# A hybrid convolution and gMLP trunk on eight cores: another DMA queue for cached weights, write-backs in mid-use, a norm pipelined with mixer A, conv weights on VectorE

## The chip, the cores and the metric

The program runs on all 8 cores of one Trainium2 chip; each core works on its own 4096 tokens, and nothing is exchanged between cores. The metric is the device time of the slowest core, in microseconds (us). Executions in a slow state (one die, cores 0 to 3 or 4 to 7, at a lower granted clock, or a run over 1.5% above the fastest of its kernel) are set aside; only fast runs are compared. TensorE is called PE.

A core does its tokens in four passes (0 to 3) of 1024. A pass has a layer 0 mixer, an MLP, a layer 1 mixer and an MLP. The weights, 45 pieces of 1 MB in bf16, come through a ring of four slots in every pass. The first load of a piece is a cast load: GpSimd issues a DMA that reads 2 MB of float32 and writes 1 MB of bf16. The piece is then written back to a bf16 cache in device memory, and later loads take it from there.

Four marks are used throughout; unless said otherwise each is the median of the eight cores in the profiled execution:

- *conv end*: the last matmul of mixer A's convolution in pass 0
- *late stretch*: from the first matmul of layer 0's output projection in pass 0 to the first projection matmul of pass 1
- *pass 0 end*: that first projection matmul of pass 1
- *pass 1 stretch*: from there to pass 1's own layer 0 output projection

## The reference, cut to what matters

```python
def conv_mixers(h, w_in, ...):                      # layer 0
    z = h @ w_in                                    # one projection, 2560 columns
    a = a_val * sigmoid(a_gate)                     # A: GLU
    a = silu(layer_norm(causal_depthwise_conv(a, conv_a_w) + conv_a_b))   # width 31
    bo = b_gate * causal_depthwise_conv(c_gate * b_val, conv_b_w)         # B
    return concatenate([a, bo]) @ w_out
for i in range(2):
    h = h + mixer_i(rms_norm(h))                    # layer 0 above, layer 1 gMLP
    h = h + squared_relu_mlp(rms_norm(h))
return rms_norm(h)
```

## The kernel before

The kernel records every operation with what it reads and writes; waits follow from that record, and each engine runs its own operations in order. SyncE issues all DMAs except the cast loads.

```python
NEV = 7
def wb_mt(i):                       # pass in which piece i is written back
    return 1 if i % NPIECE < NEV else 0     # layer 0's seven "ev" pieces: pass 1
def issue(i, gate=()):
    ...
    if i // NPIECE > wb_mt(i):      # from the cache, SyncE
        P.op("sp", ... dma_start(out=ring[s], in_=wcache[...]), ...)
        return
    P.op("pool", ... dma_start(out=ring[s], in_=src), reads=list(gate), ...)   # cast load
def take(expect):                   # first use of a piece
    ...
    if i // NPIECE == wb_mt(i) and ...:
        P.op("sp", ... dma_start(out=wcache[...], in_=ring[s]), ...)           # write-back
def release(i):                     # a slot's last use is past
    issue(i + NSLOT)
...
# mixer A, group m: two token halves, then an exchange through device memory
def a_glu(m):
    for s in range(2):
        bg = fm_group(slot, cb, s); bv = fm_group(slot, cb + 1, s)    # 8 matmuls each
        ... sigmoid on ScalarE, product on VectorE into abuf[m % 2] ...
    P.op("sp", ... dma_start(out=scr_a[m]..., in_=ab.v...), dma=f"a{m}")        # store
    P.op("sp", ... dma_start(out=A4.v[...], in_=scr_a[m]...), dma=f"b{m}")      # load
...
for m in range(4):
    a_glu(m)
    if mt == 0:
        for g in range(8 + 2 * m, 10 + 2 * m): gen_cw("dve", g)   # conv weights 8 to 15
    if m % 2 == 1: release(a_pc[m // 2][0])                       # loads pieces 4 and 5
for gp in range(NG // 2): conv_pair(gp)                           # conv on PE
...   # B mixer; the normalised A output goes through scr_s the same way (4 stores)
...
for k in range(1, NSLOT):            # start: pieces 1 to 3
    issue(k, h_keys(2 * k + 1))      # each after an x tile has landed
    for g in range(3 * k - 3, min(3 * k, 8)): gen_cw("pool", g)   # conv weights 0 to 7
```

The first norm runs over all eight token tiles before the first projection; each tile's transpose comes two tiles after its scaling (LAG = 2). In both exchanges a store to device memory is followed by a load in another order; the loads of the later one (scr_s) are called gathers.

Of the kernel before, what the change touches and what calls it, by code (L numbers as in the profile page):

```python
# [18 lines left out]
NTB = 8  # L19
# [196 lines left out]
def build_program(n_mt=4):  # L216
# [16 lines left out]
    NPIECE = 45  # L233
    NEV = 7
    wcache = nc.dram_tensor("wcache", [NPIECE, 128, 8 * 512], BF16, kind="Internal").ap()

    P = Prog()
    with contextlib.ExitStack() as es:
# [93 lines left out]

        def wb_mt(i):
            return 1 if i % NPIECE < NEV else 0

        def issue(i, gate=()):
            if i >= len(pieces):
                return
            assert i == issued[0]
            issued[0] += 1  # L340
            wn, r0, c0 = pieces[i]
            s = i % NSLOT
            if i // NPIECE > wb_mt(i):
                src = wcache[i % NPIECE].rearrange("p (kc n) -> p kc n", kc=8)
                P.op("sp", lambda e, s=s, src=src: e.dma_start(out=ring[s][:], in_=src),
                     reads=[("wc", i % NPIECE)], writes=[("w", s)], dma=f"v{s}")
                return
            src = W[wn][r0:r0 + 1024, c0:c0 + 512].rearrange("(kc p) n -> p kc n", p=128)
            P.op("pool", lambda e, s=s, src=src: e.dma_start(out=ring[s][:], in_=src),
                 reads=list(gate), writes=[("w", s)], dma=f"w{s}")  # L350

        def take(expect):
            i = cur[0]
            assert pieces[i] == expect, (pieces[i], expect)
            assert i < issued[0], (i, issued[0])
            cur[0] += 1
            s = i % NSLOT
            if i // NPIECE == wb_mt(i) and i + NPIECE < len(pieces):
                dst = wcache[i % NPIECE].rearrange("p (kc n) -> p kc n", kc=8)
                P.op("sp", lambda e, s=s, dst=dst: e.dma_start(out=dst, in_=ring[s][:]),  # L360
                     reads=[("w", s)], writes=[("wc", i % NPIECE)], dma=f"wb{s}")
            return i, s

        def release(i):
            issue(i + NSLOT)
# [24 lines left out]
        for tb in range(NTB):  # L390
            load_x(0, tb)
            if tb == 3:
                P.op("sp", lambda e: e.dma_start(out=wexp.v, in_=wexp_d.rearrange("p (g u) -> p g u", g=NG)),
                     writes=wexp.k(), dma="c1")
        P.op("sp", lambda e: e.dma_start(out=cst[:], in_=bigc[:, 0:2048]), writes=[("cst",)], dma="c2")

# [9 lines left out]

        def gen_cw(eng, g):
            small(eng, lambda e: e.tensor_tensor(
                out=cw[:, g, :].rearrange("p (u c) -> p u c", c=32),
                in0=mask32.v.unsqueeze(1).to_broadcast([128, NLAG * NPH, 32]),  # L410
                in1=wexp.v[:, g, :].unsqueeze(2).to_broadcast([128, NLAG * NPH, 32]), op=ALU.mult),
                mask32.k() + wexp.ki(g), [("cw", g)])
# [57 lines left out]

        LAG = 2
        xn_done = [False]
# [6 lines left out]
        def xn_op(c0, tb, eng="act", src=h_tile, dst=xn_tile):  # L479
            (ap, keys), (out, okeys) = src(tb), dst(tb)  # L480
            col = st[:, c0 + 8 + tb:c0 + 9 + tb]
            if eng == "act":
                small("act", lambda e: e.activation(out=out, in_=ap, func=AF.Copy, scale=col),  # L483
                      keys + [("st", c0 + 8 + tb)], okeys)
            else:
                small("dve", lambda e: e.tensor_scalar(out=out, in0=ap, scalar1=col, scalar2=None, op0=ALU.mult),
                      keys + [("st", c0 + 8 + tb)], okeys)
# [46 lines left out]
        def norm_to_xnT(nidx):  # L534
# [3 lines left out]
            c0 = stcol(16)  # L538
            for tb in range(3):
                stat_tb(c0, tb)  # L540
            LATE = 6
            for tb in range(NTB):
                if tb >= LAG:
                    tr_op(nidx, tb - LAG)
                if tb >= LATE:
                    stat_tb(c0, tb)
                rstd_tb(c0, tb)
                if tb + 3 < LATE:
                    stat_tb(c0, tb + 3)
                xn_op(c0, tb, "act" if tb % 2 == 0 else "dve")  # L550
            for tb in range(NTB - LAG, NTB):
                tr_op(nidx, tb)

        pre_c0 = [0]
# [114 lines left out]
        def fm_group(slot, m, s):  # L669
# [4 lines left out]
            def mm(e):  # L674
# [3 lines left out]
                return r  # L678
            P.op("pe", mm, reads=[("w", slot)] + [("xnT", tb) for tb in range(4 * s, 4 * s + 4)], writes=[("ps", b)])
            pump()  # L680
            return b

        def tm_group(slot, lhs, lhs_keys, tb):
            b = next_bank()

            def mm(e):
# [3 lines left out]
                return r  # L690
            P.op("pe", mm, reads=[("w", slot)] + lhs_keys, writes=[("ps", b)])
            return b

# [43 lines left out]
        def mixer0(mt):  # L737
# [8 lines left out]

            def a_glu(m):
                ab = abuf[m % 2]
                slot = a_pc[m // 2][1]
                cb = 2 * (m % 2)  # L750
                for s in range(2):
                    bg = fm_group(slot, cb, s)
                    bv = fm_group(slot, cb + 1, s)
                    sg = gbuf[s]
                    small("act", lambda e, bg=bg, sg=sg: e.activation(out=sg.v, in_=banks[bg][:], func=AF.Sigmoid),
                          [("ps", bg)], sg.k())
                    small("dve", lambda e, bv=bv, sg=sg, ab=ab, s=s: e.tensor_tensor(
                        out=ab.v.rearrange("p (j q t) -> p j q t", j=NPH, q=2)[:, :, s, :],
                        in0=banks[bv][:].rearrange("p (j t) -> p j t", j=NPH),
                        in1=sg.v.rearrange("p (j t) -> p j t", j=NPH), op=ALU.mult),  # L760
                        [("ps", bv)] + sg.k(), [k for j in range(NPH) for k in ab.k(j * TP + s * 128, j * TP + s * 128 + 128)])
                P.op("sp", lambda e, ab=ab, m=m: e.dma_start(
                    out=scr_a[m].rearrange("(i c) (d t) -> (c d) i t", i=NPH, d=4),
                    in_=ab.v.rearrange("p (i t) -> p i t", i=NPH)), reads=ab.k(), writes=[("scra", m)], dma=f"a{m}")
                P.op("sp", lambda e, m=m: e.dma_start(
                    out=A4.v[:, 4 * m:4 * m + 4, HB:HB + TP], in_=scr_a[m].rearrange("p (d t) -> p d t", d=4)),
# [142 lines left out]

            for m in range(4):  # L910
                a_glu(m)
                if mt == 0:
                    for g in range(8 + 2 * m, 10 + 2 * m):
                        gen_cw("dve", g)
                if m % 2 == 1:
                    release(a_pc[m // 2][0])
            for gp in range(NG // 2):
                conv_pair(gp)
                if mt > 0 and gp >= 2:
                    load_x(mt, gp - 2)  # L920
# [130 lines left out]
        for k in range(1, NSLOT):  # L1051
            issue(k, h_keys(2 * k + 1))
            for g in range(3 * k - 3, min(3 * k, 8)):
                gen_cw("pool", g)
        for mt in range(n_mt):
# [71 lines left out]
```

## Time and profile before

| | before |
|---|---|
| three runs before the prediction | 2749.64 us median (2747.91 to 2750.39) |
| PE busy, slowest core | 2645.0 of 2745.2 us |
| first projection matmul, conv end | 49.2, 97.7 us |
| late stretch, pass 0 end | 573.2, 719.9 us (714.2 to 733.8) |
| pass 1 stretch | 108.5 us |

The profiled core is the slowest, core 1. The first lines of its page:

```profile
span 2745.2 us, 40038 instructions; the slowest of 8 cores (2726.8 to 2745.2 us)
...
PE 2645.0 (96%) x13400; PEld 1261.3 (46%) x13400; DVE 1062.3 (39%) x1949; ACT 905.5 (33%) x1625; POOL 714.3 (26%) x691
```

PE is the bottleneck; a change that leaves its own work as it is can win only its 100 idle us. The windows view tells where they are. Its columns are the window, its length, then busy time and count of PE, PE weight loads, VectorE, ScalarE and GpSimd, then PE's granted clock, DMA share and GB/s:

```profile
0.00:200.00 200.00, 141.01 (x759) 73.46 (x760) 111.54 (x158) 70.63 (x126) 42.14 (x41) 0.95 0.63 121
...
700.00:900.00 200.00, 180.32 (x985) 91.40 (x984) 108.08 (x165) 71.93 (x134) 34.12 (x29) 0.97 0.61 161
1380.00:1600.00 220.00, 215.34 (x1161) 107.81 (x1159) 116.39 (x181) 75.44 (x139) 33.87 (x29) 1.00 0.37 125
```

The start loses 59 us (200 less 141), the mixer of pass 1 20, the same mixer of pass 2 only 5. The timeline of PE shows what it waited for (start, length, instruction, and in brackets the idle time before it and its releaser):

```profile
50.01 29.07 PE L676 MATMUL bank<-xnT,ring 128*128 128x512 bf16 x128
78.91 11.99 PE L776 MATMUL bank<-Z,cw 128*128 128x256 bf16 x108
93.41 5.76 PE L776 MATMUL bank<-Z,cw 128*128 128x256 bf16 x36 [2.51 <-DMA Z<-scr_a]
...
163.04 8.09 PE L626 MATMUL bank<-ring,Z 128*128 128x512 bf16 x24 [10.27 <-DMA Z<-scr_s]
...
771.93 6.18 PE L776 MATMUL bank<-Z,cw 128*128 128x256 bf16 x36 [10.29 <-DMA Z<-scr_a]
```

Mixer A's projections run without a break from 50.0 to 78.9, conv waits 2.5 us for the exchange, the output projection of pass 0 waits 10.3 us for the second exchange (scr_s), and conv of pass 1 waits 10.3 us. One VectorE operation in the first norm stands out in the timeline:

```profile
27.13 11.39 DVE L486 TENSOR_SCALAR xn_tm<-h,st 128x1024 bf16<-128x1024 f32 x1
```

The same operation elsewhere takes 0.75 us. GpSimd was building conv weights meanwhile. Here is the exchange of mixer A, groups 0, 1 and 3, in SyncE's timeline. A load into Z waits for its store to land, so the distance from a store's line to its load's line is the time of the store:

```profile
59.31 0.38 SPq L762 DMA_DIRECT2D scr_a<-Z  x1
61.75 0.61 SPq L765 DMA_DIRECT2D Z<-scr_a  x1
66.20 0.38 SPq L762 DMA_DIRECT2D scr_a<-Z  x1
71.70 0.53 SPq L765 DMA_DIRECT2D Z<-scr_a  x1
...
80.12 0.56 SPq L762 DMA_DIRECT2D scr_a<-Z  x1
90.11 0.53 SPq L765 DMA_DIRECT2D Z<-scr_a  x1
```

A store of 256 KB took 2.4 us once and 10.0 us another time. GpSimd's timeline has a cast load issued just ahead of the slow one:

```profile
79.63 0.87 POOL L349 DMA_DIRECT2D ring<-ev_w_out  x1 [12.88 <-PE bank L676]
```

### The profile page before, as it was taken

The page shows a single profiled execution, that of the slowest core. Times are in us where ns is not written, and L with a number is a line of the kernel's source. Part 1 is how long each engine was busy: PE and PEld are TensorE (multiplying, and loading weights), DVE is VectorE, ACT ScalarE, POOL GpSimd, SP SyncE. Part 2 cuts the span into 40 slices and gives each one's busy share as a digit, 9 for nine tenths or more (in the row PEclk, how much of TensorE's full clock was granted, in tenths as well). Part 3 has the DMA queues.
Part 4 walks back from the last instruction along what each step waited for, and adds up shares of the span by engine and source line. Part 5 has one row for each costly group of instructions (what it writes and reads, how often), then busy time and mean ns, then how long its engine had stood idle before and what let it go on. Part 6 is the DMA issues. An engine that isn't in the chain of part 4 may idle for free.

```text
span 2745.2 us, 40038 instructions; the slowest of 8 cores (2726.8 to 2745.2 us)
## 1 busy us (share of the span) xinstructions
PE 2645.0 (96%) x13400; PEld 1261.3 (46%) x13400; DVE 1062.3 (39%) x1949; ACT 905.5 (33%) x1625; POOL 714.3 (26%) x691
## 2 busy tenths in 40 slices
PE   3989999999979999999999999999999999999998
PEld 2534444444444444444445444444445444445443
DVE  4641226421455123732157321462125721265223
ACT  2432135423334113532323412552333422164112
POOL 3115322323211322222311223123320133203222
PEclk9999999999999999999999999999999999999999
DMA  7567765978774211223244112122326222212212
GB/s 155 85 135 149 156 140 124 188 163 166 173 181 158 76 63 71 84 93 116 82 143 166 62 67 88 62 86 101 107 77 214 80 91 77 77 62 77 77 62 93
DMA packets 128681, 303.89 MB, mean 111 GB/s; under 512 B 22880, under 2 KB 92512, under 8 KB 106208
## 3 DMA queue, kind: packets, MB, share of 16 engines
q1 hardware_dynamic: 74400, 246.79, 25.2%
q0 software_dynamic: 54080, 54.53, 14.3%
q8 instruction: 112, 1.84, 0.3%
q14 instruction: 89, 0.73, 0.1%
HBM read 283.47 MB, written 72.35 MB: 130 GB/s over the span
## 4 chain that ended last, share of the span: by engine, by line
PE 89%; DMA 4%; DVE 3%; issue 3%; ACT 1%; SPq 0%; DVEq 0%; ACTq 0%
PE bank L688 42%; PE bank L676 41%; DMA scr_a<-Z 2%; PE bank L496 2%; PE bank L776 2%; PE bank L626 1%; DMA scr_s<-Z 1%; DMA h<-x 1%; DVE Z L896 1%; DMA Z<-scr_s 1%; PE bank L998 1%; DVE Z L826 0%; DVE Z L905 0%; DMA Z<-scr_a 0%; DVE Z L824 0%
## 5 line engine op out<-in xcount | busy, mean ns | idle before, releaser
L676 PE MATMUL bank<-xnT,ring 128*128 128x512 bf16 x5888 | 1291.3, 380 | 11.4 <-DVE Z L905 8.5
L688 PE MATMUL bank<-ring,Z 128*128 128x512 bf16 x4928 | 1080.8, 379 | 0.0
L695 DVE TENSOR_TENSOR h<-bank,h 128x512 f32<-128x512 f32 x640 | 439.6, 690 | 1399.5 <-PE bank L688 1358.8
L676 PEld LDWEIGHTS bank<-xnT,ring 128*128 128x128 bf16 x5888 | 574.1, 98 | 698.2 <-issue 23.2
L726 POOL TENSOR_TENSOR Z<-Z 128x512 bf16<-128x512 f32 x512 | 531.3, 1039 | 1104.4 <-ACT Z L724 1104.2
L688 PEld LDWEIGHTS bank<-ring,Z 128*128 128x128 bf16 x4928 | 479.2, 98 | 565.2
L724 ACT ACTIVATE Z<-bank 128x512 f32<-128x512 f32 x512 | 304.3, 597 | 1108.6 <-PE bank L676 1091.7
L467 ACT ACTIVATE junk<-h 128x1024 bf16<-128x1024 f32 x136 | 142.0, 1044 | 147.1 <-DVE h L695 136.8
L483 ACT ACTIVATE xn_tm<-h,st 128x1024 bf16<-128x1024 f32 x100 | 114.6, 1146 | 106.3 <-DVE st L515 100.1
L508 DVE TENSOR_TENSOR xnT<-bank,sm 128x1024 bf16<-128x1024 bf16 x96 | 115.5, 1217 | 3.8 <-PE bank L496 3.3
L688 PE MATMUL bank<-ring,xnT 128*128 128x512 bf16 x512 | 115.1, 379 | 0.0
L496 PE MATMUL bank<-ident,xn_tm 128*128 128x128 bf16 x928 | 72.0, 225 | 44.0 <-ACT st L522 25.5
L496 PEld LDWEIGHTS bank<-ident,xn_tm 128*128 128x128 bf16 x928 | 61.1, 100 | 71.6 <-issue 53.7
L776 PE MATMUL bank<-Z,cw 128*128 128x256 bf16 x576 | 68.3, 282 | 15.1 <-DMA Z<-scr_a 13.2
L522 ACT ACTIVATE st<-st 128x1 f32<-128x1 f32 x160 | 31.0, 194 | 151.0 <-DVE st L515 123.8
L970 POOL TENSOR_TENSOR st<-st,mhalf 128x1 f32<-128x1 f32 x32 | 17.6, 549 | 236.8 <-DVE st L968 236.8
L688 PEld LDWEIGHTS bank<-ring,xnT 128*128 128x128 bf16 x512 | 49.4, 98 | 56.6
L1006 DVE SCALAR_TENSOR_TENSOR Z<-bank,sm,biasT 128x128 f32<-128x128 f32 x256 | 68.9, 339 | 12.5 <-PE bank L998 12.2
L776 PEld LDWEIGHTS bank<-Z,cw 128*128 128x128 bf16 x576 | 57.8, 101 | 26.0 <-issue 16.8
L1011 POOL TENSOR_TENSOR Z<-Z 128x512 bf16<-128x512 f32 x44 | 50.4, 1158 | 62.4 <-DVE Z L1006 62.4
L626 PE MATMUL bank<-ring,Z 128*128 128x512 bf16 x192 | 45.0, 396 | 19.2 <-DMA Z<-scr_s 10.3
L952 DVE TENSOR_TENSOR Z<-bank,cst 128x512 f32<-128x512 f32 x64 | 44.1, 689 | 41.2 <-PE bank L688 30.9
(89 smaller groups left out, 1005.4 us busy)
## 6 DMA issues: line engine op xcount, KB each, us to landing
ring<-wcache SPq DMA_DIRECT2D x128, 1024.0 KB, 4.9
wcache<-ring SPq DMA_DIRECT2D x45, 1024.0 KB, 8.3
h<-x SPq DMA_DIRECT2D x32, 512.0 KB, 10.6
ring<-w_0 POOLq DMA_DIRECT2D x16, 1024.0 KB, 13.6
ring<-w_1 POOLq DMA_DIRECT2D x16, 1024.0 KB, 14.8
y<-Z SPq DMA_DIRECT2D x32, 512.0 KB, 2.8
Z<-x SPq DMA_DIRECT2D x24, 512.0 KB, 5.4
ring<-ev_w_in POOLq DMA_DIRECT2D x10, 1024.0 KB, 18.0
```

The source lines that it names most:

```text
L467: small("act", lambda e: e.activation(out=junk[:], in_=ap, func=AF.Square, accum_out=st[:, c0 + tb:c0 + tb + 1]), keys, [("st", c0 + tb), ...
L483: small("act", lambda e: e.activation(out=out, in_=ap, func=AF.Copy, scale=col), keys + [("st", c0 + 8 + tb)], okeys)
L496: r = e.transpose(tbk[:, kc * 128:(kc + 1) * 128], xt[:, kc * 128:(kc + 1) * 128], ident[:])
L508: small("dve", lambda e: e.tensor_tensor(out=xnT[:, :, tb * 128:(tb + 1) * 128], in0=tbk.rearrange("p (k n) -> p k n", k=8), in1=gcol.unsq ...
L626: r = e.matmul(banks[b][:], lhsT=lhs(kc, tb), rhs=ring[slot][:, kc, :], start=(kc == 4), stop=(kc == 3))
L676: r = e.matmul(banks[b][:], lhsT=ring[slot][:, kc, m * 128:(m + 1) * 128], rhs=xnT[:, kc, s * 512:(s + 1) * 512], start=(kc == 0), stop=(k ...
L688: r = e.matmul(banks[b][:], lhsT=lhs(kc, tb), rhs=ring[slot][:, kc, :], start=(kc == 0), stop=(kc == 7))
L695: small("dve", lambda e: e.tensor_tensor(out=h[:, tb, d * 512:(d + 1) * 512], in0=banks[b][:], in1=h[:, tb, d * 512:(d + 1) * 512], op=ALU ...
L724: small("act", lambda e, b=b, rb=rb: e.activation(out=rb.v, in_=banks[b][:], func=AF.Relu), [("ps", b)], rb.k())
L726: small("pool", lambda e, rb=rb, hq=hq, c=c, s=s: e.tensor_tensor(out=hq.v[:, c, s * 512:(s + 1) * 512], in0=rb.v, in1=rb.v, op=ALU.mult), ...
L776: r = e.matmul(banks[b][:, half_ * TP:(half_ + 1) * TP], lhsT=cw[:, g, L * 128:(L + 1) * 128], rhs=A4.v[:, g, HB - L:HB - L + TP], start=( ...
L1006: r = e.scalar_tensor_tensor(out=sv.v[:, j * 128:(j + 1) * 128], in0=banks[b][:, j * 128:(j + 1) * 128], scalar=sm[:, SM_LNGV + g:SM_LNGV ...
```

## The change

Its intent: start PE on the first token half while the second is still being normalised; take the conv weights off GpSimd; hold the first weight pieces back so that x lands first; move cached loads and write-backs to ScalarE's queue; write every piece back in pass 0, so that pass 1 needs no cast loads.

```diff
-    NEV = 7
...
-            if i // NPIECE > wb_mt(i):
+            if i >= NPIECE:
...
-                P.op("sp", lambda e, s=s, src=src: e.dma_start(out=ring[s][:], in_=src),
+                P.op("act", lambda e, s=s, src=src: e.dma_start(out=ring[s][:], in_=src),
...
-            if i // NPIECE == wb_mt(i) and i + NPIECE < len(pieces):   # write-back at take, SyncE
+            if i < NPIECE < len(pieces):
+                wb_left[s] = [2, i]
+        def used(s):                      # called after each matmul group
+            ...                           # the second one issues the write-back
+                P.op("act", lambda e, s=s, dst=dst: e.dma_start(out=dst, in_=ring[s][:]), ...)
...
-                small("dve", lambda e: e.tensor_scalar(out=out, in0=ap, scalar1=col, ...
+                small("dve", lambda e: e.tensor_tensor(out=out, in0=ap, in1=col.to_broadcast([128, 1024]), op=ALU.mult),
...
-            for tb in range(NTB):         # first norm: transposes two tiles behind
-                if tb >= LAG:
-                    tr_op(nidx, tb - LAG)
-                ...
+            def tile(tb):
+                if tb + 1 < NTB:
+                    stat_tb(c0, tb + 1)
+                    rstd_aff(c0, tb + 1)
+                rstd_sqrt(c0, tb)
+                rstd_rcp(c0, tb)
+                xn_op(c0, tb, "act" if tb % 2 == 0 else "dve")
+                tr_op(nidx, tb)
+            for tb in range(4):
+                tile(tb)
+            for tb in range(4, NTB):      # one after each matmul group
+                pend.append(lambda tb=tb: tile(tb))
...
+            if mt == 0:
+                order[:4] = [(0, 0), (1, 0), (0, 1), (1, 1)]     # (group, token half)
+            for m, s in order:
+                a_half(m, s)
+                if mt == 0:
+                    for _ in range(1 if m < 2 else 3):
+                        gen_cw(gen.pop(0))                       # all 16 on VectorE
+                if s == 1:
+                    a_send(m)                                    # store and load
+                    if m % 2 == 1:
+                        release(a_pc[m // 2][0])
...
-            issue(k, h_keys(2 * k + 1))
+            issue(k, h_keys(6) if k == 1 else [("w", k - 1)])
```

Also, the table of conv weights is loaded earlier and a constant table later.

More of the change, by code (lines that the diff above doesn't have):

```diff
@@ L331, in build_program @@
         issued = [0]
-        def wb_mt(i):
-            return 1 if i % NPIECE < NEV else 0
         def issue(i, gate=()):
@@ L357, in take @@
             s = i % NSLOT
-            if i // NPIECE == wb_mt(i) and i + NPIECE < len(pieces):
-                dst = wcache[i % NPIECE].rearrange("p (kc n) -> p kc n", kc=8)
-                P.op("sp", lambda e, s=s, dst=dst: e.dma_start(out=dst, in_=ring[s][:]),
-                     reads=[("w", s)], writes=[("wc", i % NPIECE)], dma=f"wb{s}")
+            if i < NPIECE < len(pieces):
+                wb_left[s] = [2, i]
             return i, s
+        wb_left = {}
+        def used(s):
+            if s not in wb_left:
+                return
+            wb_left[s][0] -= 1
+            if wb_left[s][0] == 0:
+                i = wb_left.pop(s)[1]
+                dst = wcache[i].rearrange("p (kc n) -> p kc n", kc=8)
+                P.op("act", lambda e, s=s, dst=dst: e.dma_start(out=dst, in_=ring[s][:]),
+                     reads=[("w", s)], writes=[("wc", i)], dma=f"wb{s}")
         def release(i):
@@ L391, in build_program @@
             load_x(0, tb)
-            if tb == 3:
+            if tb == 0:
                 P.op("sp", lambda e: e.dma_start(out=wexp.v, in_=wexp_d.rearrange("p (g u) -> p g u", g=NG)),
                      writes=wexp.k(), dma="c1")
-        P.op("sp", lambda e: e.dma_start(out=cst[:], in_=bigc[:, 0:2048]), writes=[("cst",)], dma="c2")
         def build_masks():
@@ L405, in build_masks, with gen_cw @@
                 small("dve", lambda e, ps=ps: e.memset(blk[ps, ps], 1.0), [("blk",)], [("blk",)])
-        def gen_cw(eng, g):
-            small(eng, lambda e: e.tensor_tensor(
+        def gen_cw(g):
+            small("dve", lambda e: e.tensor_tensor(
                 out=cw[:, g, :].rearrange("p (u c) -> p u c", c=32),
@@ L469, in stat_tb @@
                   keys, [("st", c0 + tb), ("junk",)])
-        LAG = 2
         xn_done = [False]
@@ L485, in xn_op @@
             else:
-                small("dve", lambda e: e.tensor_scalar(out=out, in0=ap, scalar1=col, scalar2=None, op0=ALU.mult),
+                small("dve", lambda e: e.tensor_tensor(out=out, in0=ap, in1=col.to_broadcast([128, 1024]), op=ALU.mult),
                       keys + [("st", c0 + 8 + tb)], okeys)
@@ L538, in norm_to_xnT @@
             c0 = stcol(16)
-            for tb in range(3):
-                stat_tb(c0, tb)
-            LATE = 6
-            for tb in range(NTB):
-                if tb >= LAG:
-                    tr_op(nidx, tb - LAG)
-                if tb >= LATE:
-                    stat_tb(c0, tb)
-                rstd_tb(c0, tb)
-                if tb + 3 < LATE:
-                    stat_tb(c0, tb + 3)
+            def tile(tb):
[4 more added lines that the diff above has]
+                rstd_rcp(c0, tb)
                 xn_op(c0, tb, "act" if tb % 2 == 0 else "dve")
-            for tb in range(NTB - LAG, NTB):
                 tr_op(nidx, tb)
+            stat_tb(c0, 0)
+            rstd_aff(c0, 0)
+            for tb in range(4):
+                tile(tb)
+            for tb in range(4, NTB):
+                pend.append(lambda tb=tb: tile(tb))
         pre_c0 = [0]
@@ L679, in fm_group @@
             P.op("pe", mm, reads=[("w", slot)] + [("xnT", tb) for tb in range(4 * s, 4 * s + 4)], writes=[("ps", b)])
+            used(slot)
             pump()
@@ L691, in tm_group @@
             P.op("pe", mm, reads=[("w", slot)] + lhs_keys, writes=[("ps", b)])
+            used(slot)
             return b
@@ L745, in mixer0, with a_half @@
                 small("pool", lambda e: e.tensor_copy(out=A4.v[:, :, 0:HB], in_=halo_a[:]), [("halo_a",)], A4.k() + a4k)
-            def a_glu(m):
+            def a_half(m, s):
                 ab = abuf[m % 2]
@@ L750, in a_glu, with a_send @@
                 cb = 2 * (m % 2)
-                for s in range(2):
-                    bg = fm_group(slot, cb, s)
-                    bv = fm_group(slot, cb + 1, s)
-                    sg = gbuf[s]
-                    small("act", lambda e, bg=bg, sg=sg: e.activation(out=sg.v, in_=banks[bg][:], func=AF.Sigmoid),
-                          [("ps", bg)], sg.k())
-                    small("dve", lambda e, bv=bv, sg=sg, ab=ab, s=s: e.tensor_tensor(
-                        out=ab.v.rearrange("p (j q t) -> p j q t", j=NPH, q=2)[:, :, s, :],
-                        in0=banks[bv][:].rearrange("p (j t) -> p j t", j=NPH),
-                        in1=sg.v.rearrange("p (j t) -> p j t", j=NPH), op=ALU.mult),
-                        [("ps", bv)] + sg.k(), [k for j in range(NPH) for k in ab.k(j * TP + s * 128, j * TP + s * 128 + 128)])
-                P.op("sp", lambda e, ab=ab, m=m: e.dma_start(
+                bg = fm_group(slot, cb, s)
+                bv = fm_group(slot, cb + 1, s)
+                sg = gbuf[(m + s) % 2]
+                small("act", lambda e: e.activation(out=sg.v, in_=banks[bg][:], func=AF.Sigmoid), [("ps", bg)], sg.k())
+                small("dve", lambda e: e.tensor_tensor(
+                    out=ab.v.rearrange("p (j q t) -> p j q t", j=NPH, q=2)[:, :, s, :],
+                    in0=banks[bv][:].rearrange("p (j t) -> p j t", j=NPH),
+                    in1=sg.v.rearrange("p (j t) -> p j t", j=NPH), op=ALU.mult),
+                    [("ps", bv)] + sg.k(), [k for j in range(NPH) for k in ab.k(j * TP + s * 128, j * TP + s * 128 + 128)])
+            def a_send(m):
+                ab = abuf[m % 2]
+                P.op("sp", lambda e: e.dma_start(
                     out=scr_a[m].rearrange("(i c) (d t) -> (c d) i t", i=NPH, d=4),
                     in_=ab.v.rearrange("p (i t) -> p i t", i=NPH)), reads=ab.k(), writes=[("scra", m)], dma=f"a{m}")
-                P.op("sp", lambda e, m=m: e.dma_start(
+                P.op("sp", lambda e: e.dma_start(
                     out=A4.v[:, 4 * m:4 * m + 4, HB:HB + TP], in_=scr_a[m].rearrange("p (d t) -> p d t", d=4)),
@@ L908, in b_gate @@
                         op=ALU.mult), [("ps", b)] + cc_.k(), mixT.k((4 + m) * T + s * 512, (4 + m) * T + (s + 1) * 512))
-            for m in range(4):
-                a_glu(m)
-                if mt == 0:
-                    for g in range(8 + 2 * m, 10 + 2 * m):
-                        gen_cw("dve", g)
-                if m % 2 == 1:
-                    release(a_pc[m // 2][0])
+            order = [(m, s) for m in range(4) for s in range(2)]
+            gen = list(range(NG))
+            if mt == 0:
+                order[:4] = [(0, 0), (1, 0), (0, 1), (1, 1)]
+            for m, s in order:
+                a_half(m, s)
+                if mt == 0:
+                    for _ in range(1 if m < 2 else 3):
[4 more added lines that the diff above has]
+                        release(a_pc[m // 2][0])
             for gp in range(NG // 2):
                 conv_pair(gp)
+                if mt == 0 and gp == 4:
+                    P.op("sp", lambda e: e.dma_start(out=cst[:], in_=bigc[:, 0:2048]), writes=[("cst",)], dma="c2")
                 if mt > 0 and gp >= 2:
@@ L1051, in build_program @@
         for k in range(1, NSLOT):
-            issue(k, h_keys(2 * k + 1))
-            for g in range(3 * k - 3, min(3 * k, 8)):
-                gen_cw("pool", g)
+            issue(k, h_keys(6) if k == 1 else [("w", k - 1)])
         for mt in range(n_mt):
```

## The prediction

> **What bounds it.** The page gives TensorE (PE) 2645 us busy of 2745.2 (96%); the chain that ended last is 89% PE. At most about 100 us of PE idleness can be won. By windows PE loses about 47 us in 0 to 200; under 1 in 200 to 700; 20 in 700 to 900 (layer 0 mixer of pass 1); 5 in that mixer of passes 2 and 3 each; 11 at the end. The other cores agree.
>
> **Start.** Timeline: projection matmuls begin at 50.0 us. The first norm does all eight tiles first; one VectorE scaling (tensor_scalar, elsewhere 0.75 us) took 11.39 us, from 27.1 to 38.5, while GpSimd built eight conv weights of 2.1 us each, ending 37.8. The Trainium skill ("GPSIMD Engine Reference", overview table) says the engines share SBUF interfaces and contend with VectorE's 2-port modes; this trace agrees. Weight piece 0 lands at about 27 us, sharing the DMA engines with x.
>
> The change builds all 16 weights on VectorE (1.31 us each), scales with tensor_tensor (I estimate 1.2 us), and starts with tokens 0 to 511. Tile 3's chain needs x tile 4 (lands about 22 us): stat 1.25, root and reciprocal 0.5, scale 1.2, transpose 1.0, eviction 1.2: about 27 us, just as piece 0 lands. Four groups of 1.73 us interleave with tiles 4 to 7; the second token half begins near 38. Piece 1, held until x tile 6 has landed (about 27), lands at 40 to 43. Mixer A ends near 60, not 79. VectorE gives some back: in the last four half groups 3 x 1.31 + 0.69 = 4.6 us per 3.46 us of PE. The scratch exchange (2.4 to 10 us per store, 3 to 6 per load) stays serial on SyncE, behind a GpSimd memset that now waits for piece 2. Conv ends at 78 to 84 instead of 99: **gain 18 us** (12 to 23).
>
> **Rest of pass 0.** Seven more 1 MB write-backs fall here. Before, PE waited 10.3 us for the last gather of the normalised A output, then ran at a granted 0.78 clock (160 to 180 us). More write traffic may lengthen this, a separate queue may help; I take 0 (plus or minus 6).
>
> **Pass 1.** Before, seven cast loads of f32 weights and seven write-backs fall here; two exchange stores took 19.7 and 12.1 us instead of about 5, and PE waited 10.3, 1.8 and 0.4 us at the conv, then ran partly slower (its first 36 conv matmuls 6.2 us against 4.1). After, this mixer should look like pass 2's, losing 5 us (VectorE waits at the b gating, untouched): **gain 16 us** (13 to 18).
>
> **The ScalarE queue.** An issue costs about 0.32 us on SyncE; 173 on ScalarE make 55 us where it is a third busy, and each release comes after ScalarE has waited for about the same PE group anyway. PE shows no waits for ring loads in passes 1 to 3, so earlier issue buys nothing by itself. Effect: 0 (minus 2 to plus 4).
>
> **Sum.** 2749.6 - 18 - 16 = about 2715 us. Range 2699 to 2729. Within 2% most likely (2% would need 55 of the 100 idle us).
>
> **What would show it.** First projection matmul at 26 to 30 us; the 11.4 us scaling gone; last mixer A matmul at 57 to 64; B projections from 78 to 84; PE idle in the pass 1 mixer 5 to 7 us; f32 input-projection loads 5 rather than 10; passes 2 and 3 unchanged to 1 us.
>
> **What would make it wrong.** Pieces 1 or 2 landing after 50 or 65 us, now chained one behind the other; VectorE overload making conv wait; write-backs slowing the pass 0 gathers by over 10 us; ScalarE blocked by an issue's wait so that evictions hold PE's banks.

## The result, and the profile after

The time was 2732.57 us median of 4 runs (2728.67 to 2734.19), against 2748.77 before (2744.12 to 2750.39). A ratio quoted here is the mean time of one kernel's fast runs over that of the other's in the same rounds, so it is not quite the ratio of the medians; it was 0.9942, 95% interval 0.9925 to 0.9959. The kernel got faster by 0.6%, half of what I foretold, and outside my range.

The slowest core was now core 2. Its page and windows:

```profile
span 2730.4 us, 39950 instructions; the slowest of 8 cores (2717.9 to 2730.4 us)
...
PE 2645.3 (97%) x13400; PEld 1260.4 (46%) x13400; DVE 1061.8 (39%) x1957; ACT 907.5 (33%) x1627; POOL 689.0 (25%) x676
```

```profile
0.00:200.00 200.00, 141.41 (x755) 72.69 (x756) 113.17 (x166) 72.16 (x127) 24.52 (x33) 0.94 0.67 143
...
700.00:900.00 200.00, 195.21 (x1067) 98.67 (x1066) 111.14 (x173) 73.61 (x136) 30.70 (x26) 1.00 0.41 137
1380.00:1600.00 220.00, 214.44 (x1130) 106.17 (x1129) 108.14 (x169) 76.48 (x140) 39.12 (x33) 0.99 0.37 125
```

The whole gain is in the second line: pass 1's mixer loses 5 us instead of 20, as foretold. The first 200 us hold 141.4 us of PE work, where they held 141.0. PE's timeline answers why:

```profile
31.23 3.57 PE L681 MATMUL bank<-xnT,ring 128*128 128x512 bf16 x8 [1.48 <-DVE st L531]
...
49.43 22.37 PE L681 MATMUL bank<-xnT,ring 128*128 128x512 bf16 x96 [1.48 <-DVE xnT L512]
76.80 5.54 PE L784 MATMUL bank<-Z,cw 128*128 128x256 bf16 x36 [5.00 <-DMA Z<-scr_a]
85.73 13.65 PE L784 MATMUL bank<-Z,cw 128*128 128x256 bf16 x108 [3.39 <-DMA Z<-scr_a]
...
164.79 7.17 PE L631 MATMUL bank<-ring,Z 128*128 128x512 bf16 x24 [9.46 <-DMA Z<-scr_s]
...
762.55 15.94 PE L784 MATMUL bank<-Z,cw 128*128 128x256 bf16 x144
```

PE starts 19 us earlier, is done with mixer A at 71.8 instead of 79.1, and then waits: conv ends at 99.4, before at 99.2. Pass 1's conv (last line) now runs through. The second token half starts only at 49.4. In VectorE's timeline the first norm is a chain, one tile every 3.9 us:

```profile
18.10 1.22 DVE L512 TENSOR_TENSOR xnT<-bank,sm 128x1024 bf16<-128x1024 bf16 x1 [2.69 <-PE bank L500]
...
22.05 1.23 DVE L512 TENSOR_TENSOR xnT<-bank,sm 128x1024 bf16<-128x1024 bf16 x1 [1.27 <-PE bank L500]
...
25.91 1.22 DVE L512 TENSOR_TENSOR xnT<-bank,sm 128x1024 bf16<-128x1024 bf16 x1 [2.51 <-PE bank L500]
```

Each eviction (L512) waits for its tile's transpose on PE, and VectorE takes up the next tile's reciprocal (the last step of its root) only after it. SyncE's exchange and GpSimd's cast loads:

```profile
55.48 0.38 SPq L770 DMA_DIRECT2D scr_a<-Z  x1
71.10 0.62 SPq L773 DMA_DIRECT2D Z<-scr_a  x1
71.81 0.56 SPq L770 DMA_DIRECT2D scr_a<-Z  x1
77.27 0.53 SPq L773 DMA_DIRECT2D Z<-scr_a  x1
77.89 0.69 SPq L770 DMA_DIRECT2D scr_a<-Z  x1
86.22 0.53 SPq L773 DMA_DIRECT2D Z<-scr_a  x1
...
132.60 1.15 SPq L850 DMA_DIRECT2D scr_s<-Z  x1
147.33 0.92 SPq L854 DMA_DIRECT2D Z<-scr_s  x2
```

```profile
52.95 0.87 POOL L345 DMA_DIRECT2D ring<-ev_w_in  x1 [11.47 <-DMA ring<-ev_w_in]
...
58.59 0.87 POOL L345 DMA_DIRECT2D ring<-ev_w_in  x1 [4.55 <-PE bank L681]
...
130.88 0.91 POOL L345 DMA_DIRECT2D ring<-w_0  x1 [12.93 <-DMA wcache<-ring]
```

The first store took 15.6 us, where it took 2.4 before; a cast load had been issued 2.5 us ahead of it. The store at 132.6 took 14.7 us, 1.7 us behind another cast load.

Over the cores the picture is harder still (medians):

| | before | after |
|---|---|---|
| first projection matmul | 49.2 | 30.6 |
| last transpose of the norm ends | 49.3 | 47.5 |
| conv end | 97.7 | 96.9 |
| late stretch | 573.2 | 582.5 |
| pass 0 end | 719.9 | 728.2 |
| pass 1 stretch | 108.5 | 90.8 |

On the median core pass 0 got *longer* by 8 us, and pass 1 gave back 18. The slowest core hides this: before, that was core 1, which already waited 10.3 us at pass 0's output projection and ended pass 0 at 733.8; now core 2 ends it at 734.8. Before, only cores 1 and 3 had a late stretch above 575 us (586.3 and 581.4); now all eight have 581.8 to 586.3. For the slowest cores the account of the spans is +1.1 to the end of pass 0, -17.8 in the pass 1 stretch, +1.9 from there to the end: -14.8 us (2745.2 to 2730.4).

### The profile page after: what moved, and what is told of

It reads as the page before. It is cut to its first block, busy times and chain, and to the rows that moved or that the text cites. A ratio compares the mean times of both kernels' runs of the same rounds, so it can differ in the third digit from the quotient of the medians.

```text
span 2730.4 us, 39950 instructions; the slowest of 8 cores (2717.9 to 2730.4 us)
## 1 busy us (share of the span) xinstructions
PE 2645.3 (97%) x13400; PEld 1260.4 (46%) x13400; DVE 1061.8 (39%) x1957; ACT 907.5 (33%) x1627; POOL 689.0 (25%) x676
## 4 chain that ended last, share of the span: by engine, by line
PE 90%; DVE 3%; DMA 3%; issue 3%; ACT 0%; SPq 0%; DVEq 0%; ACTq 0%
PE bank L694 43%; PE bank L681 41%; PE bank L500 2%; PE bank L784 2%; PE bank L631 1%; DMA scr_s<-Z 1%; DMA scr_a<-Z 1%; DVE Z L904 1%; PE bank L1014 1%; DMA Z<-scr_a 0%; DMA h<-x 0%; DVE Z L832 0%; DVE Z L834 0%; DVE Z L913 0%; DVE Z L901 0%
## 5 line engine op out<-in xcount | busy, mean ns | idle before, releaser
L512 DVE TENSOR_TENSOR xnT<-bank,sm 128x1024 bf16<-128x1024 bf16 x96 | 115.5, 1216 | 19.1 <-PE bank L500 19.1
L694 PEld LDWEIGHTS bank<-ring,xnT 128*128 128x128 bf16 x512 | 49.4, 98 | 56.7
## 6 DMA issues: line engine op xcount, KB each, us to landing
h<-x SPq DMA_DIRECT2D x32, 512.0 KB, 11.1
```

The source lines that it names most:

```text
L512: small("dve", lambda e: e.tensor_tensor(out=xnT[:, :, tb * 128:(tb + 1) * 128], in0=tbk.rearrange("p (k n) -> p k n", k=8), in1=gcol.unsq ...
L694: r = e.matmul(banks[b][:], lhsT=lhs(kc, tb), rhs=ring[slot][:, kc, :], start=(kc == 0), stop=(kc == 7))
```

## The experiments

The theories at the start were W (the seven write-backs now in pass 0 slow the exchange) and L (the first weight pieces, held back and chained, now load at the time of the exchange). The chip fell into the slow state often during these runs, so totals have wide intervals. "Total" is the median of a kernel's fast runs. Each run was also correct against the reference.

### Write the ev pieces back in pass 1 again

```diff
+        def wb_mt(i):
+            return 1 if i % NPIECE < 7 else 0
-            if i >= NPIECE:
+            if i // NPIECE > wb_mt(i):
-            if i < NPIECE < len(pieces):
+            if i // NPIECE == wb_mt(i) and i + NPIECE < len(pieces):
```

> The changed kernel, but the seven ev pieces (input and output projection of layer 0) are again loaded by cast in pass 1 and written back there, as before the change; queue and mid-use issue stay. Marks, median of the 8 cores: conv of pass 0 ends at 96.9 us in the changed kernel, pass 0 ends (first projection matmul of pass 1) at about 728 us (720 before the change), pass 1 from there to its output projection takes 91 us (108 before). Theory W (the seven write-backs now in pass 0 slow the scratch exchange and eat the startup gain): first exchange store 2 to 6 us on most cores instead of 7 to 16, conv ends by 90, pass 0 ends at 706 to 714, pass 1 stretch back at 105 to 109; total about 2732 (2726 to 2738). Rival L (the chained cast loads, landing later, do it): conv still ends at 96 to 99, pass 0 ends at 726 to 730, pass 1 stretch 105 to 109; total about 2748.

Measured: conv end 94.7, late stretch 575.2, pass 0 end 718.0, pass 1 stretch 108.8; total 2744.0 of 3 fast runs (ratio 0.9981, 0.9838 to 1.0123). W is half right: without the write-backs the late stretch is nearly back to normal, and the first store took 2.3 to 4.3 us on all cores, as W foretold; but the second now took 4.9 to 11.6, and conv gains only 2 us. L is not confirmed either. The pass 1 stretch is fully back at its old length, with the ScalarE queue still in use: the queue is not what made pass 1 faster.

### The old gates for the first pieces

```diff
-            issue(k, h_keys(6) if k == 1 else [("w", k - 1)])
+            issue(k, h_keys(2 * k + 1))
```

> The changed kernel with the old gates of weight pieces 1 to 3 (after x tiles 3, 5, 7 instead of after tile 6 and then one behind the other). Theory L: pieces 2 and 3 are out of the way by 50 us, the first exchange store takes at most 6 us on all cores, conv ends by 90, pass 0 ends by 720, total about 2724. Theory W: the write-backs are unchanged, so conv ends at 95 to 99 and the total stays within 4 us of 2732. Under both the first projection matmul comes 0 to 5 us later, as x shares the DMA engines.

Measured: conv end 94.5 (92.0 to 96.8), late stretch 582.1, pass 0 end 725.3; total 2731.2 (ratio 0.9951, 0.9771 to 1.0132). L falls in the form it had. The first store now took 2.5 to 3.1 us on every core, as L said, but conv did not follow: on the five cores where conv ended latest the *second* store took 10.8 to 13.8 us, and it was issued 0.5 to 0.7 us behind piece 4's cast load. On the other three it was issued 0.33 us behind that load and took 5.0 to 5.1 us.

### Each half of the change alone

Queue and write-backs alone: the kernel before with the first four hunks of the diff and the two calls of `used`. The start alone: the kernel before with all other hunks.

> The kernel before, with only the ScalarE queue, the write-backs of all pieces in pass 0 and their mid-use issue; norm, conv weights and gates as before. Theory W: projections start at 48 to 50, conv ends at 96 to 104, pass 0 ends near 729 to 735 (9 to 15 later than before), pass 1 stretch 91; total about 2740. Rival (write-backs harmless, the new start is what costs in pass 0): pass 0 ends at 718 to 722, total about 2731.

> The kernel before, with only the new start (norm pipelined by token half, gates chained, conv weights on VectorE, order of the A groups, later table load); SyncE queue and write-backs as before. Theory W: without write-backs in pass 0 the start pays: conv ends at 84 to 90, pass 0 ends at 706 to 712, pass 1 stretch 108; total about 2737. Rival (the start by itself gains nothing, its chained loads or its serial norm lose it again): conv ends at 95 to 99, pass 0 ends at 718 to 724, total 2746 to 2752.

| | conv end | late stretch | pass 0 end | pass 1 stretch | total |
|---|---|---|---|---|---|
| before | 97.7 | 573.2 | 719.9 | 108.5 | 2751.7 |
| queue and write-backs alone | 99.6 | 582.5 | 732.6 | 90.8 | 2733.5 |
| start alone | 94.0 | 574.8 | 718.5 | 110.6 | 2743.4 |
| both (the change) | 96.9 | 582.5 | 728.2 | 90.8 | 2732.6 |

(Totals of before and of the halves are of one set of rounds; ratios 0.9915, 0.9822 to 1.0009, and 0.9947, 0.9855 to 1.0039.) Queue and write-backs carry the pass 1 gain and the loss of 9 us in the late stretch, so in the first half W holds (pass 0 end 732.6, foretold 729 to 735). The start is worth about 3 us at conv end (97.7 to 94.0, and 99.6 to 96.9), although PE begins 18 us sooner, and this holds *without* write-backs in pass 0. So W does not explain the lost start: it foretold 84 to 90, and the rival's total (2746 to 2752) missed too.

### A third theory: a store behind a fresh cast load

I then listed every exchange store of pass 0 on all cores of the six kernels run so far, with the DMAs issued around it (cast loads from 13 us ahead, write-backs from 6 us ahead, both until the store had landed; the table has 123 of the 384 stores, those in other constellations are left out):

| issued around the store | stores | median us | range |
|---|---|---|---|
| nothing | 23 | 2.4 | 2.4 to 4.3 |
| a write-back, no cast load | 7 | 2.9 | 2.5 to 3.0 |
| a cast load 0.5 to 3.5 us ahead | 93 | 11.1 | 6.2 to 17.3 |

The gap matters. Read from the same traces afterwards (issue to landing): the 93 stores of the last row landed 0.3 us (median) after their cast load, but 49 stores issued less than 0.5 us behind one, while its issuing instruction (0.9 us) was still running, took 5.0 us (median; 2.9 to 11.2) and landed 7.6 us before it (the slow store shown before the change, 0.49 us behind, is among the longest of them). Why half a us makes this difference stays open.

A cast load took 9.1 us with no other DMA of its core in flight (median of 28), 11.2 with nothing but the exchange beside it (139). Theory P: a store issued just after a cast load crawls until about the end of that load. Both are released by the same matmul group's end, so they meet again and again. Theory N: the unlagged norm chain delays the second token half by 8 us, but while the exchange binds, that cannot be seen.

### SyncE's queue instead of ScalarE's

```diff
-                P.op("act", lambda e, s=s, src=src: e.dma_start(out=ring[s][:], in_=src),
+                P.op("sp", lambda e, s=s, src=src: e.dma_start(out=ring[s][:], in_=src),
```

and the same for the write-back.

> The changed kernel with all cached loads and write-backs put on SyncE's queue again. Theory M (the pass 1 gain comes from the loads and write-backs that left pass 1, not from the queue): pass 1 stretch stays at 90 to 93 us (108 before), total 2728 to 2740. Rival Q (the separate queue is what frees the exchange in pass 1): pass 1 stretch 98 or more, total 2742 or more.

Measured: pass 1 stretch 90.9, conv end 97.6, pass 0 end 721.3, total 2728.7 (ratio 0.9929, 0.9909 to 0.9948). M holds: the queue by itself buys nothing; the kernel is as fast or a little faster without it. The Trainium skill ("DMA: Bandwidth & Descriptors", section "Issuing engines are not separate DMA queues") says that DMAs of all issuing engines run on the same 16 DMA engines and that spreading them saves only issue time; this run agrees. The late stretch was 574.6 although all write-backs were in pass 0: a possible reason, not tested by itself, is that in SyncE's order they came later, and with them the cast loads into those slots (piece 7 issued at 134.8, median, instead of 128.6). The third store of the later exchange had no cast load ahead of it there and took 5.1 us (median of the cores; 13.3 in the changed kernel).

### The norm pipelined again

```diff
-                tr_op(nidx, tb)           # inside tile(tb)
-            for tb in range(4):
+            tile(0)
+            for tb in range(1, 5):
                 tile(tb)
+                tr_op(nidx, tb - 1)
-                pend.append(lambda tb=tb: tile(tb))
+                pend.append(lambda tb=tb: ((tile(tb + 1) if tb + 1 < NTB else None), tr_op(nidx, tb)))
```

> The changed kernel with the first norm software pipelined again: each tile's transpose and eviction one tile behind its scaling, same token halves. Theory N (the unlagged norm is a serial chain of 4 us per tile and delays the second token half): last transpose of the norm ends at 38 to 42 us instead of 47.5, first projection at 26 to 29. If the exchange beside the cast loads (theory P) is what binds after that, conv still ends at 92 to 98 and the total is within 5 us of 2732; if the norm is what binds, conv ends at 86 to 90 and the total is near 2724.

Measured: last transpose at 40.4 (47.5), first projection at 27.1 (30.6), as N says; conv end 94.5 (91.3 to 98.5), total 2733.0 (ratio 0.9952, 0.9933 to 0.9972). Of 7 us gained in the norm, 2.4 were left at conv end: the second store took 12.9 to 17.8 us on all cores. The exchange binds.

### Cast loads of pieces 4 and 5 held until mixer A's exchange has landed

With the old gates, so that nothing else loads then:

```diff
-                    if m % 2 == 1:
+                    if m % 2 == 1 and mt > 0:
                         release(a_pc[m // 2][0])
+            if mt == 0:
+                for i, slot in a_pc:
+                    release(i, a4k)       # gate: all of the exchange has landed
```

> The early gates of the second run, and in pass 0 the cast loads of pieces 4 and 5 held until the scratch exchange of mixer A has landed. Theory P (an exchange store issued just after a cast load crawls until that load is done: 2 to 3 us alone, 8 to 15 us beside it): no store of mixer A takes over 5 us, last one issued at 72 to 76, conv ends at 84 to 89 on all cores (94.5 with early gates alone), total 2718 to 2726. Rival: the stores stay at 5 to 13 us because the write-back of piece 1 or other cores' traffic slows them, conv ends at 92 or later.

Measured: every A store 2.3 to 4.4 us; conv end 86.4 (85.1 to 87.0 on the eight cores), against 94.5 with the old gates alone; total 2721.7 (ratio 0.9910, 0.9886 to 0.9934). P holds and its rival falls: the write-back of piece 1 still runs beside the first two stores. SyncE's timeline of the slowest core, the second and fourth A stores and the third of the later exchange:

```profile
58.81 0.89 SPq L770 DMA_DIRECT2D scr_a<-Z  x1
62.27 0.53 SPq L773 DMA_DIRECT2D Z<-scr_a  x1
...
74.98 0.36 SPq L770 DMA_DIRECT2D scr_a<-Z  x1
77.33 0.53 SPq L773 DMA_DIRECT2D Z<-scr_a  x1
...
120.84 0.45 SPq L850 DMA_DIRECT2D scr_s<-Z  x1
132.54 0.91 SPq L854 DMA_DIRECT2D Z<-scr_s  x2
```

and from its GpSimd timeline the cast load ahead of the third:

```profile
119.90 0.91 POOL L345 DMA_DIRECT2D ring<-w  x1 [14.08 <-PE bank L681]
```

The A stores take 3.5 and 2.4 us; the store at 120.8, which has the next cast load (issued at 119.9) ahead of it, 11.7. So part of the gain is given back: the late stretch is 584.4, and pass 0 ends at 721.0, only 4.3 us sooner than with the old gates alone, though conv ended 8.1 sooner.

### Cast loads of pieces 7 and 8 held until the later exchange has landed

```diff
-                            [("scrs", m)], mixT.k(...), dma=f"t{m}")
+                            [("scrs", m)], mixT.k(...) + [("gath", m)], dma=f"t{m}")
-                    release(b_pc[b_rel[0]][0])
+                    release(b_pc[b_rel[0]][0], [("gath", m) for m in range(4)] if mt == 0 and b_rel[0] > 0 else ())
-                    b_release(min(m, 2))
+                    b_release(min(m, 2) if mt > 0 else 1)
```

> The changed kernel; in pass 0 the cast loads of pieces 7 and 8 (first MLP weights) held until the last gather of the normalised A output has landed. Theory P: stores of that exchange 2 to 6 us, no wait at the output projection, so the stretch from its start to pass 1 is 573 to 575 us instead of 582 to 586, total about 2724. Rival W2 (the write-back of piece 4, which stays, is what slows it): the stretch stays at 580 or more, total about 2732.

Measured on the changed kernel: late stretch 574.1 (582.5), pass 0 end 721.3, total 2725.8 (ratio 0.9927, 0.9911 to 0.9944). P holds; W2 falls. Together with the first experiment this says that on the median core the loss in the late stretch needs both: cast loads without write-backs cost 2 us (575.2), write-backs without cast loads 1 (574.1), both 9. On single cores cast loads alone can do it: without the write-backs two of eight still had 582.4 and 582.9. How the two join is read from the kept traces, not shown by a run. The third store had a cast load 0.9 to 2.3 us ahead of it on every core before the change too, and took 9.9 us (median of the cores); in the changed kernel, where the write-back of piece 4 was in flight beside it on every core, it took 13.3. The last gather landed 0.7 us (median) after the output projection had begun before the change, and 12 us after in the changed kernel.

### Everything together, and two parts taken out

Old gates, both holds, the pipelined norm, and two conv weights after every half group.

> All together on the changed kernel: early gates, pieces 4 and 5 held until the A exchange has landed, pieces 7 and 8 held until the last gather, norm pipelined one tile deep, two conv weights per half group. Theory P plus N: last transpose of the norm at 39 to 43 us, every exchange store 2 to 6 us, conv ends at 77 to 82, no wait at the output projection (stretch to pass 1 573 to 576), pass 0 ends at 700 to 706 (728 in the changed kernel), pass 1 stretch 91, total 2703 to 2711, about 1.5% under the kernel before. If something else binds (a held load arriving late, VectorE), conv or the first MLP shows a new wait and the total stays above 2715.

> The same without the pipelined norm (the changed kernel's serial one). With the exchange free, theory N makes the norm bind: last transpose at 47 to 50, conv ends at 85 to 88, total 6 to 9 us above the kernel with everything.

> The same as the kernel with everything, but conv weights one per half group and then three, as in the change. If VectorE's bundles of three matter (4.6 us of VectorE per 3.46 us of PE), the last exchange store starts 2 to 5 us later and conv ends 1 to 4 us later; if PE's own conv work hides them, the total is equal within 3 us.

| | last transpose | conv end | pass 0 end | total |
|---|---|---|---|---|
| everything | 41.8 | 81.9 | 706.5 | 2716.1 |
| without the pipelined norm | 49.0 | 87.2 | 712.2 | 2720.8 and 2726.1 |
| conv weights 1 and 3 per half group | 40.3 | 81.2 | 704.8 | 2715.4 |

(Everything: ratio 0.9877, 0.9859 to 0.9895. The second row had only two fast runs. The third: 0.9872, 0.9857 to 0.9886.) N holds once the exchange is free: the norm chain costs 5 us at conv end and still 6 at the end of pass 0. The bundles of three conv weights, of which I had feared that they would overload VectorE, cost nothing: the last A store starts 2 us later (about 69 instead of 67) and PE's conv work hides it.

Pass 0 ended 22 us sooner than in the changed kernel, at 706.5 (foretold 700 to 706), but the total missed its band of 2703 to 2711. PE's waits after pass 0 on the slowest core of the kernel with everything:

```profile
PE bank L632 <- DVE Z L914: 8.4, 3, 2.9
PE bank L785 <- DMA Z<-scr_a: 6.2, 2, 4.8
PE bank L682 <- DVE Z L914: 5.8, 3, 2.0
PE bank L632 <- DMA Z<-scr_s: 2.3, 1, 2.3
```

The columns are total, times and longest. The two waits for exchange data were 0 to 1.6 us together on any core of the changed kernel; here they are 3.2 to 8.5, and 1.4 to 10.2 in the third row's kernel.

### Where those last microseconds went

Two candidates: cached loads on ScalarE's queue beside the exchange of passes 1 to 3, or the cores, which now reach their exchanges within about 4 us of each other (14 in the changed kernel). Both kernels are the last row above with SyncE's queue; the second also issues the two cached loads that mixer A frees behind the exchange in every pass:

```diff
-                    if m % 2 == 1 and mt > 0:
-                        release(a_pc[m // 2][0])
-            if mt == 0:
-                for i, slot in a_pc:
-                    release(i, a4k)
+            for i, slot in a_pc:
+                release(i, a4k if mt == 0 else ())
```

> The kernel with held loads and pipelined norm (conv weights one, then three per half group), with cached loads and write-backs on SyncE's queue. If cached loads on a second queue beside the exchange cause the late waits, PE's waits for exchange data after pass 0 fall from 5 to 9 us to under 3 us and the total to 2704 to 2710 (2715 with ScalarE's queue). If it is the cores' closeness in time, waits and total stay (2711 to 2719).

> The same on SyncE's queue, and in every pass the two cached loads that mixer A releases are issued behind the last exchange store and load. If cached loads beside the exchange are the cause even on one queue, this removes the last of them: no exchange wait at the conv in passes 1 to 3, total 2703 to 2708. Otherwise equal to the run before within 3 us.

With SyncE's queue alone the waits for exchange data after pass 0 were 0 to 3.9 us per core, total 2711.7 of 4 fast runs (0.9872, 0.9838 to 0.9905): above the first band and at the lower edge of the second, and the ratio is that of ScalarE's queue, so this run does not decide. (Its profiled execution had two cores at a clock of 0.984 and 0.985, so its marks are not used; on the undisturbed die the waits were also 0 to 3.9.) With the loads behind the exchange, the waits are 0 to 0.4 us and the total is 2706.7 of 4 fast runs (2705.3 to 2707.7), ratio 0.9836 (0.9811 to 0.9861) against 2750.5 in the same rounds. The same view of its slowest core, complete:

```profile
PE bank L632 <- DVE Z L914: 8.4, 3, 2.9
PE bank L682 <- DVE Z L914: 5.8, 3, 2.0
PE bank L500 <- ACT st L526: 0.6, 3, 0.2
```

No wait for exchange data is left. The cores were as close in time (pass 0 ends between 703.9 and 708.0), so closeness is not the cause; large cached loads beside the exchange are. This kernel beats the one before by 1.6% and the changed one by about 1% (0.9836 over 0.9942, from different rounds). No run parts what in a large load does it: its size, the cast or the queue.

## Why the prediction was wrong

- **Size and sign.** Foretold -34 us (2715), measured -16 (2732.6). Faster by less than 2% was right; the range (2699 to 2729) missed by 4 us.
- **Pass 1, "gain 16 us": right, with its reason.** The stretch fell by 17.7 us (108.5 to 90.8) and the mixer loses what pass 2's does. The old length came back with the loads and write-backs in pass 1, although ScalarE's queue stayed (108.8), and did not come back on SyncE's queue (90.9).
- **The ScalarE queue, 0: right for the total, but not harmless.** The run on SyncE's queue is no slower (2728.7). It had a late stretch of 574.6 where ScalarE's queue had 582.5, and with pass 0 mended, cached loads on it beside the exchange came with waits of 1.4 to 10.2 us, which moving them to SyncE's queue and behind the exchange removed.
- **Start, "conv ends at 78 to 84 instead of 99: gain 18 us": this step failed.** Conv ended at 96.9 on the median core, 0.8 sooner than before. Two terms of the sum were wrong. First, "the second token half begins near 38": it began at 48 to 49, and mixer A ended at 71.0 on the median core instead of near 60, because I followed one tile's chain from the landing of x and assumed that tiles would overlap. The change had dropped the lag, and each tile takes 3.9 us in series. With the lag restored the norm ended at 40.4, and this was worth 5 us once it could be seen. Second, "the scratch exchange (2.4 to 10 us per store) stays serial": I wrote down the spread and used its comfortable middle. The changed order puts the stores of groups 0 and 1 close to the cast loads of pieces 3 and 4, where the slower of the two takes 6 to 16 us, by core. Mended alone, the exchange is the larger of the two: the pipelined norm brought conv end to 94.5, the old gates with held loads to 86.4. Both mends brought it to 81.2, the time I had foretold.
- **"Rest of pass 0 ... I take 0 (plus or minus 6)": failed as well.** The late stretch grew by 9 us on the median core. "A separate queue may help" was wrong: with the same write-backs on SyncE's queue it was 574.6. For the slowest core it hardly shows, because before the change that core already had this wait.
- **What I had listed as dangers.** Pieces 1 and 2 landed at 40.6 and 53 us in the slowest core, inside my limits; VectorE's overload was harmless; ScalarE was not blocked (PE's waits for it after 60 us are 0.8 to 3.2 us per core, before 0.8 to 3.7). Write-backs did slow the late stretch, with cast loads. The danger that came true, cast loads meeting the exchange, was not on my list. It was in the trace of before: its fourth A store took 10.0 us, right behind the load issued at 79.63.
- **GpSimd and VectorE.** The 11.4 us scaling disappeared as foretold. The Trainium skill ("GPSIMD Engine Reference", section "1. Specifications") says that GpSimd shares its SBUF interfaces with VectorE, and contends with VectorE's 2-port modes and with its instructions that have two SBUF inputs; the trace before agrees (11.39 us for 0.75). The change altered both the form of the scaling (now 1.23 us) and GpSimd's work, and no run parts the two. Freeing this wait moved the bottleneck to the norm chain and the exchange.

## What to carry to other kernels

Where one DMA's time varies by a factor of four in a profile, find out what is issued next to it before costing a change that moves it: here a small store 0.5 to 3.5 us behind a large cast load took 11.1 us instead of 2.4. Large prefetches with slack are better gated on the landing of the small exchange that PE is about to need than on the event that frees their buffer, since here that event sends the exchange too. When work is started earlier, look at every later station (norm chain, exchange, next exchange) for the one that now binds, and read all cores: the slowest core alone hid that pass 0 had become longer.

## What the Trainium skill lacked or had wrong

- "DMA: Bandwidth & Descriptors", section "Queues, rings and completion order", says that a DMA engine takes turns between its queues, packet by packet. It does not say what that leaves of a small transfer behind a fresh large one on another queue: 256 KB stores took 11.1 us (median of 93) with a 1 MB cast load issued 0.5 to 3.5 us ahead, 5.0 us (49) with one issued less than 0.5 us ahead, 2.9 us (7) beside a write-back of 1 MB, and 2.4 us (23) alone.
- No page that I used advises holding a prefetch until an exchange has landed; it was worth 8 us at conv end in pass 0 (94.5 to 86.4).
- "GPSIMD Engine Reference", section "1. Specifications", names the contention with VectorE without a size (other pages of the skill have more on it and were not used here): a 0.75 us scaling took 11.39 us, past five conv weights that GpSimd built one after the other in 2.1 us each.
- "ScalarE: Activation LUTs", section "What ACT_TABLE_LOAD costs", gives about 1283 ns for a table load and about 1380 ns for a drain that comes with it, 2.66 us in all. Every table load in the traces of before and after that I read takes 1.28 us, as the page says, but the drain does not show: at 37.81 us in the changed kernel the instruction before the load ends, at 39.12 the next begins. The interleaving of norm and mixer A raised their number in the first 120 us from 4 to 6.
